# Layer 1's gate and up projections: seven block products in place of eight, from the fourth tile on

## The chip, the cores and the metric

One core of one Trainium2 chip runs the whole program in one launch. The metric is device microseconds of one execution; lower is better. The kernel before takes 1570.13 us (median of three runs, 1569.8 to 1570.21).

## What is computed

Two layers of a bidirectional backbone over 512 latent tokens (and, in layer 0, 256 context tokens), width 1024, all in f32. The change touches only the feed-forward block of layer 1, which works on the 512 latent tokens alone. Cut to that:

```python
D_MODEL, SEQ, D_FF = 1024, 512, 2816

def conv_ffn(h, w_gate, w_up, conv_w, conv_b, w_down):
    g = dwconv(h @ w_gate, conv_w, conv_b, FFN_CONV // 2, FFN_CONV // 2)   # 3 taps along the tokens
    return (jax.nn.silu(g) * (h @ w_up)) @ w_down

# layer 1, the last one
x   = layer_norm(ALPHA * x + m_x[2] * y_x, ln1_g[1], ln1_b[1])
f_x = conv_ffn(modulate(x, m_x[3], m_x[4]), ffn_w_gate[1], ffn_w_up[1], ffn_conv_w[1], ffn_conv_b[1], ffn_w_down[1])
x   = layer_norm(ALPHA * x + m_x[5] * f_x, ln2_g[1], ln2_b[1])
```

## The kernel before, in words

Matrix products keep f32 accuracy by splitting each operand into a high and a low part in a reduced f32 format and adding three products (high by high, high by low, low by high): `mm3`, lines 327 to 329. The activations of layer 1's feed-forward block are `h1h` and `h1l`, 128 partitions by 8 slices (k) by 512 tokens. Weights are loaded as f32 into `raw` (three buffers), cast to the high part on ScalarE (L146), and the low part is got by a subtraction on VectorE (L147); `wh` and `wl` have four buffers each. `units` is the list of weight panels in the order of their use; `split_to` and `use` walk it, and `dma_to` issues the loads on SyncE's queue in that order. The down panels are also multiplied by a row vector on VectorE (L152) before they are split (L153, L154).

The feed-forward block is cut into 22 tiles (t) of 128 hidden channels. A tile needs one gate panel and one up panel of 8 slices. In layer 1 each is one accumulation of 8 x 3 matmuls of 512 columns (`proj`), followed by the convolution over the tokens (two VectorE operations of 511 columns, L947 and L948, after a ScalarE copy out of PSUM, L946), Silu (L949), the product with up (L1776) and the split of the result into `a1` (L1703, L1704). Tiles are gathered in groups of 4, 4, 4, 4, 2 and 4 (`FG1`); the order `order2` is f0 to f4, down of group 0, f5 to f8, down of group 1, and so on, and last f19, f20, f21 and the down of group 5. A down of four tiles is eight accumulations of 4 x 3 matmuls of 512 columns, each added to the residual `R` on VectorE (L1792).

Before tile 0 stands the layer norm of the second half of the tokens, SB (`ln1_1(SB)`). While it runs, TensorE works on panels for the first half of the tokens (256 columns, `first_half`): six panels, those of tiles 0, 1 and 2. Their second halves follow when the layer norm's results are there.

Layer 0 has computed its gate and up projections by seven block products since tile 3 (`SW0 = 3`, `seven_tile`, L1119): the gate and up panels, each cut into two halves of the slices, are a 2 x 2 matrix of blocks, the activations, cut into two halves of the slices and two of the tokens, are another, and seven products of sums and differences of blocks give what eight products give. There a token half is 384 columns. Each product is 4 x 3 matmuls; seven VectorE additions (L1134) put the products together, a ScalarE copy (L1136) takes the first out, four GpSimd additions per tile (L373 to L376) make the weight sums, and `seven_acts` makes the activation sums once. The instruction order on each engine is made by a planner that goes by the order of the program and by its own costs; SyncE's order is the program's.

Of the kernel before, what the change touches and what calls it, by code (L numbers as in the profile page):

```python
# [15 lines left out]
KT = 8  # L16
S = 512
# [13 lines left out]
SW0 = 3  # L31
NH = T // 2
# [30 lines left out]
def tile_backbone(ctx, tc, x, cx, cols, mod_w, w_in, w_out, gates, w_qkv, na_out, bias, w_gate, w_up, w_down, rows, out):  # L63
# [296 lines left out]

    def seven_units(l, t):
# [85 lines left out]
    for o in order2:  # L447
        if o[0] == "f":
            gu_units(1, o[1])
# [527 lines left out]
    def seven_acts():  # L977


        t2, t3 = ([ytile().rearrange("p a n -> p (a n)").rearrange("p (k n) -> p k n", k=4) for _ in range(2)] for _ in range(2))  # L980
        t4 = [[Tp.tile([128, T], F32R, tag="t", name="t4", bufs=12).rearrange("p (k n) -> p k n", k=2) for _ in range(2)] for _ in range(2)]
        lo, hi = slice(0, NH), slice(NH, T)

        def dst(j, q, k):
            if j == 1:
                return (hh, hl)[q][:, k, hi]
            if j == 4:
                return t4[q][k // 2][:, k % 2, :]
            return (t2, t3)[j - 2][q][:, k, :]

        t1 = f(ytile().rearrange("p a n -> p (a n)").rearrange("p (k n) -> p k n", k=4))
        for k in range(4):
            fa, fb = Tt("fa"), Tt("fb")
            tt(out=fa, in0=f(hh[:, k, :]), in1=f(hl[:, k, :]), op=ALU.add)
            G.tensor_tensor(out=fb, in0=f(hh[:, k + 4, :]), in1=f(hl[:, k + 4, :]), op=ALU.add)
            tt(out=t1[:, k, :], in0=fa[:, hi], in1=fa[:, lo], op=ALU.subtract)
            tt(out=fa[:, hi], in0=fb[:, hi], in1=fa[:, hi], op=ALU.subtract)
            tt(out=fb[:, hi], in0=fb[:, hi], in1=t1[:, k, :], op=ALU.subtract)
# [6 lines left out]
        B["11"] = lambda q, k: (hh, hl)[q][:, k, lo]  # L1005
        B["21"] = lambda q, k: (hh, hl)[q][:, k + 4, lo]
        B["22"] = lambda q, k: (hh, hl)[q][:, k + 4, hi]
        seven["B"] = B
        yield
        for k in range(4):  # L1010
            nc.scalar.copy(dst(1, 0, k), t1[:, k, :])
            tt(out=dst(1, 1, k), in0=t1[:, k, :], in1=f(dst(1, 0, k)), op=ALU.subtract)
        yield

    seven = {}
    us = use(4, la=0)
# [23 lines left out]
    acts = seven_acts()  # L1040
# [700 lines left out]
    for u in units[state["use"] + 4:state["use"] + 6]:  # L1741
        u["pool"] = wp2
# [146 lines left out]
```

## Time and profile before

| | us |
|---|---|
| median of three runs | 1570.13 (1569.8 to 1570.21) |
| the profiled execution | 1569.22 |
| its span, first to last instruction | 1567.5 |
| TensorE busy in the span | 1528.1 (97%) |
| VectorE busy | 1158.0 (74%) |
| ScalarE busy | 766.7 (49%) |
| GpSimd busy | 320.2 (20%) |
| mean granted TensorE clock | 0.995 of full speed |

The last layer norm before the feed-forward block of layer 1 ends near 1214 us of the span, whole tiles run from about 1229 us on, and the last matmul starts at 1559.23 us. Between 1270 and 1540 us the profile shows TensorE busy without a break. The profile counts a matmul as busy from its start to its modelled end; successive matmuls overlap, so the distance from one start to the next, not the duration, is what one costs.

### The profile page before, as it was taken

Reading aid. Unit: us, or ns where it says so; the run is one execution under the profiler, and the core shown is the slowest. Engines: PE = TensorE matmul, PEld = TensorE weight load, DVE = VectorE, ACT = ScalarE, POOL = GpSimd, SP = SyncE. Lnnn points to the kernel's source line nnn. Section 1 sums busy time; section 2 is a strip of 40 time slices with the busy share of each in tenths; the row PEclk is TensorE's granted clock in tenths of the full one; section 3 lists DMA queues with packets and bytes.
Section 4 is the critical chain, followed back from the end, with each engine's and each line's share of the span. In section 5 each row is a group of like instructions: output and inputs, shape, how many; then the busy total and the mean of one; then the engine's idle time right before and its main releaser. Section 6 shows DMA issues by size and latency. Waiting matters only on the chain.

```text
span 1567.5 us, 24579 instructions
## 1 busy us (share of the span) xinstructions
PE 1528.1 (97%) x9508; PEld 1382.8 (88%) x9508; DVE 1158.0 (74%) x2061; ACT 766.7 (49%) x1309; POOL 320.2 (20%) x288
## 2 busy tenths in 40 slices
PE   7999999999999999999997999999999999999997
PEld 5888889998999999999997998989899988888886
DVE  5665556979999989877887678886787646555567
ACT  4555664775343232424455766666757523323232
POOL 0001113411413132234143122121236000000002
PEclk9999999999999999999998999999999999999999
DMA  9743437421443525322354233441154232333331
GB/s 310 234 143 105 140 115 222 134 61 52 128 142 100 158 90 173 96 70 68 96 153 142 68 115 102 124 139 54 57 149 141 94 94 81 107 91 108 97 94 54
DMA packets 259685, 184.25 MB, mean 118 GB/s; under 512 B 6640, under 2 KB 243824, under 8 KB 259568
## 3 DMA queue, kind: packets, MB, share of 16 engines
q1 hardware_dynamic: 259568, 182.68, 38.7%
q8 instruction: 75, 1.23, 0.3%
q14 instruction: 42, 0.34, 0.1%
HBM read 180.56 MB, written 2.10 MB: 117 GB/s over the span
## 4 chain that ended last, share of the span: by engine, by line
PE 78%; DVE 11%; DMA 4%; ACT 4%; issue 2%; POOL 1%; SPq 0%; POOLq 0%; DVEq 0%; ACTq 0%
PE ps L327 20%; PE ps L329 20%; PE ps L328 20%; PE ps L1790 3%; PE ps L1788 3%; PE ps L1789 3%; DMA mw<-in_mod_w_dram 2%; DVE wl L147 2%; PE ps L258 2%; DVE wa L1102 1%; PE ps L1404 1%; DVE ma L240 1%; ACT wh L146 1%; DMA raw<-in_w_out_dram 1%; DVE X L817 1%
## 5 line engine op out<-in xcount | busy, mean ns | idle before, releaser
L146 ACT CAST wh<-raw 128x1024 fp32r<-128x1024 f32 (+3 forms) x229 | 229.4, 1005 | 359.3 <-PE ps L328 159.1
L147 DVE TENSOR_TENSOR wl<-raw,wh 128x1024 fp32r<-128x1024 f32 (+3 forms) x229 | 275.5, 1205 | 112.8 <-ACT wh L146 111.6
L327 PE MATMUL ps<-hh,wh 128*128 128x256 f32 (+2 forms) x896 | 298.8, 334 | 1.1 <-ACT hh L883 1.1
L329 PE MATMUL ps<-hh,wl 128*128 128x256 f32 (+2 forms) x896 | 297.7, 333 | 2.2 <-DVE wl L147 2.2
L328 PE MATMUL ps<-hl,wh 128*128 128x256 f32 (+2 forms) x896 | 297.3, 332 | 0.0
L327 PE MATMUL ps<-a,wh 128*128 128x256 f32 (+2 forms) x784 | 247.4, 316 | 1.1 <-ACT wh L146 1.1
L329 PE MATMUL ps<-a,wl 128*128 128x256 f32 (+2 forms) x784 | 245.4, 313 | 1.9 <-DVE wl L147 1.8
L328 PE MATMUL ps<-a,wh 128*128 128x256 f32 (+2 forms) x784 | 245.2, 313 | 0.0
L327 PEld LDWEIGHTS ps<-hh,wh 128*128 128x128 f32 x896 | 170.0, 190 | 15.6 <-issue 4.1
L329 PEld LDWEIGHTS ps<-hh,wl 128*128 128x128 f32 x896 | 170.1, 190 | 13.6 <-DVE wl L147 3.1
L328 PEld LDWEIGHTS ps<-hl,wh 128*128 128x128 f32 x896 | 170.2, 190 | 9.8
L327 PEld LDWEIGHTS ps<-a,wh 128*128 128x128 f32 x784 | 149.9, 191 | 8.9 <-ACT wh L146 2.3
L329 PEld LDWEIGHTS ps<-a,wl 128*128 128x128 f32 x784 | 149.8, 191 | 8.4 <-DVE wl L147 2.7
L328 PEld LDWEIGHTS ps<-a,wh 128*128 128x128 f32 x784 | 149.8, 191 | 5.1
L327 PE MATMUL ps<-h1h,wh 128*128 128x512 f32 (+1 forms) x400 | 146.1, 365 | 0.0
L328 PE MATMUL ps<-h1l,wh 128*128 128x512 f32 (+1 forms) x400 | 145.3, 364 | 0.1
L329 PE MATMUL ps<-h1h,wl 128*128 128x512 f32 (+1 forms) x400 | 145.3, 364 | 0.0
L1391 POOL TENSOR_SCALAR s<-s,sm 128x512 f32<-128x512 f32 x64 | 50.6, 791 | 211.1 <-DVE sm L1390 187.5
L328 PEld LDWEIGHTS ps<-h1l,wh 128*128 128x128 f32 x400 | 75.4, 189 | 12.1 <-DVE h1l L886 0.3
L329 PEld LDWEIGHTS ps<-h1h,wl 128*128 128x128 f32 x400 | 75.4, 189 | 11.9
L327 PEld LDWEIGHTS ps<-h1h,wh 128*128 128x128 f32 x400 | 75.5, 189 | 11.7
L1733 POOL TENSOR_TENSOR R<-R,gb 128x512 f32<-128x512 f32 (+1 forms) x4 | 4.8, 1196 | 340.7 <-ACT R L1732 340.7
(278 smaller groups left out, 3194.7 us busy)
## 6 DMA issues: line engine op xcount, KB each, us to landing
raw<-in_w_gate_dram SPq DMA_DIRECT2D x44, 512.0 KB, 3.9
raw<-in_w_up_dram SPq DMA_DIRECT2D x44, 512.0 KB, 3.9
mw<-in_mod_w_dram SPq DMA_DIRECT2D x40, 384.0 KB, 4.5
a<-in_mod_w_dram SPq DMA_DIRECT2D x24, 512.0 KB, 5.5
raw<-in_w_out_dram SPq DMA_DIRECT2D x24, 512.0 KB, 4.8
raw<-in_w_qkv_dram SPq DMA_DIRECT2D x24, 512.0 KB, 4.3
raw<-in_w_down_dram SPq DMA_DIRECT2D x22, 512.0 KB, 3.6
raw<-in_w_down_dram SPq DMA_DIRECT2D x24, 448.0 KB, 4.1
```

Source lines behind the costliest of these rows:

```text
L146: nc.scalar.copy(h[:, :k], raw)
L147: nc.vector.tensor_tensor(out=l[:, :k], in0=raw, in1=f(h[:, :k]), op=ALU.subtract)
L240: stt(out=a[:, 0, :], in0=w, scalar=svec[:, k, 0:1], in1=a[:, 0, :], op0=ALU.mult, op1=ALU.add)
L258: mm(ps_rows[32 * g:32 * g + 32, :], mvec[:, 4 * i + g, :], t(g), start=(i == 0), stop=(i == n - 1), tile_position=(0, 32 * g))
L327: mm(acc, wh, rh, start=first, stop=False)
L328: mm(acc, wh, rl, start=False, stop=False)
L329: mm(acc, wl, rh, start=False, stop=last)
L817: stt(out=r, in0=ps_[:, 0:e - o], scalar=lco[:, row, vec, m:m + 1], in1=r, op0=ALU.mult, op1=ALU.add)
L1391: G.tensor_scalar(out=s, in0=s, scalar1=sm[:, 2:3], scalar2=0.0, op0=ALU.mult, op1=ALU.add)
L1788: mm(p, ah, u["h"][:, k % 2, :], start=k == 0, stop=False)
L1789: mm(p, ah, u["l"][:, k % 2, :], start=False, stop=False)
L1790: mm(p, al, u["h"][:, k % 2, :], start=False, stop=k == n - 1)
```

## The change

Layer 1 gets the same seven products from tile 3 on (`SW1 = 3`), with token halves of 256 columns. The weight units of a tile become gate, up, a sum of 512 columns (`ud`) and a sum of 1024 columns (`uc`), the last two without a load. `seven_acts` is made general and is also run for layer 1, in steps between tiles 0, 1 and 2; its sums need room, so `a1` lives in two buffers `ab` whose upper third holds some of them. The convolution becomes `tail1`, run in steps between the products of the next tile. Tile 2 is no longer done by halves: four first halves stand under the layer norm in place of six, and the pool `w2` goes. In the last down, the first three slices of four accumulations are done ahead of the fourth, which needs the last tile.

```diff
+SW1 = 3
+    z_mem = [lambda: Tp.tile([128, 512], F32, tag="mr", name="z", bufs=2)]
...
-            z = Tp.tile([128, 512], F32, tag="mr", name="z", bufs=2)
+            z = z_mem[0]()
...
-            gu_units(1, o[1])
+            (gu_units if o[1] < SW1 else seven_units)(1, o[1])
...
-    def seven_acts():
+    def seven_acts(h_, n, t2, t3, t4, t1, work, seven):
...
         for k in range(4):
+            fa, fb = work("fa"), work("fb")
+            tt(out=fa, in0=f(h_[0][:, k, :]), in1=f(h_[1][:, k, :]), op=ALU.add)
+            G.tensor_tensor(out=fb, in0=f(h_[0][:, k + 4, :]), in1=f(h_[1][:, k + 4, :]), op=ALU.add)
+            tt(out=t1(k), in0=fa[:, hi], in1=fa[:, lo], op=ALU.subtract)
             tt(out=fa[:, hi], in0=fb[:, hi], in1=fa[:, hi], op=ALU.subtract)
+            tt(out=fb[:, hi], in0=fb[:, hi], in1=t1(k), op=ALU.subtract)
             tt(out=fb[:, lo], in0=fb[:, lo], in1=fb[:, hi], op=ALU.subtract)
             for j, src in ((3, fa[:, hi]), (2, fb[:, hi]), (4, fb[:, lo])):
                 nc.scalar.copy(dst(j, 0, k), src)
                 tt(out=dst(j, 1, k), in0=src, in1=f(dst(j, 0, k)), op=ALU.subtract)
             yield
...
+        for k in range(4):
+            nc.scalar.copy(dst(1, 0, k), t1(k))
+            tt(out=dst(1, 1, k), in0=t1(k), in1=f(dst(1, 0, k)), op=ALU.subtract)
         yield
...
-    tap_p = opened("tap", bufs=3, side="right")
+    tap_p = opened("tap", bufs=6, side="right")
+    t4p = opened("T4", side="right")
+    t4b = t4p.tile([128, 2, 4, 256], F32R, name="t4b")
+    z_mem[0] = lambda: t4p.tile([128, 512], F32, tag="z", name="z", bufs=1)
+    ab = [hp.tile([128, 24, 256], F32R, tag="h", name="ab") for _ in range(2)]
+    t23b = [t[:, 16:24, :].rearrange("p (q k) n -> p q k n", q=2) for t in ab]
...
-            a1[gi] = hp.tile([128, 4, 2, S], F32R, tag="h", name="a1")
+            a1[gi] = ab[gi % 2][:, 0:16, :].rearrange("p (k q h) n -> p k q (h n)", k=4, q=2)
...
-    wp2 = opened("w2", bufs=2)
...
-    pf = [bank() for _ in range(6)]
...
-    for i in range(6):
-        fillq.append(first_half(i))
+    pf = [bank() for _ in range(4)]
+    for i in range(4):
+        fillq.append(mm_seg(pf[i][:, 0:256], us[i], 0, 256, h1H, h1L, range(KT)))
...
+    def tail1(t, ga, gb_, up):
+        tap = work1("tap")
+        w = lambda k: col("fcw1", 22 * k + t)
+        for p, o in ((ga, 0), (gb_, 256)):
+            act(out=tap[:, o:o + 256], in_=p, func=AF.Identity, scale=w(1), bias=col("fcb1", t))
+        yield
+        for p, c, o, n, k in ((ga, 0, 1, 256, 0), (gb_, 0, 257, 255, 0), (ga, 1, 0, 255, 2), (gb_, 0, 255, 256, 2)):
+            stt(out=tap[:, o:o + n], in0=p[:, c:c + n], scalar=w(k), in1=tap[:, o:o + n], op0=ALU.mult, op1=ALU.add)
+            if n == 255:
+                yield
+        act(out=tap, in_=tap, func=AF.Silu)
+        yield
+        tt(out=up, in0=tap, in1=up, op=ALU.mult)
+        yield
+        ffn1_out(t, up)
+        yield
+
+    def ffn1_seven(t):
+        g, up = work1("g"), work1("up")
+        def between(i):
+            tail_step(1)
+            if t in (3, 4) and i in (1, 4):
+                run_all(x_tok(2 * t - 6 + (i > 1)))
+        ga, gb_ = seven_tile(seven1["B"], 256, g, up, between)
+        tails.append(tail1(t, ga, gb_, up))
...
-    for t in range(3):
+    for t in range(2):
+        late_step(5)
...
+        ahead(1 + t)
         ffn1_out(t, tap)
+        next(acts)
+    for it in order2[2:]:
+            if t >= SW1:
+                ffn1_seven(t)
+                continue
...
-                us = use(n // 2, la=1)
+                us = use(n // 2, la=1 + hf)
...
                     down(us, i, hf)
+                    tail_step(1)
         else:
             us = use(n)
+            part = {}
+            for i in range(2):
+                for hf in range(2):
+                    part[i, hf] = down(us[hf * (n // 2):(hf + 1) * (n // 2)], i, hf, range(n - 1))
+                    tail_step(2)
+            while tails:
+                tail_step(1)
             for i in range(4):
                 for hf in range(2):
+                    down(us[hf * (n // 2):(hf + 1) * (n // 2)], i, hf, range(n - 1, n) if (i, hf) in part else None, part.get((i, hf)))
                     final_sums(i, hf)
                 final(i)
```

## Rows read from the trace of the kernel before

**Rows 1.** The page: busy time by engine, and the chain by engine.

```profile
PE 1528.1 (97%) x9508; PEld 1382.8 (88%) x9508; DVE 1158.0 (74%) x2061; ACT 766.7 (49%) x1309; POOL 320.2 (20%) x288
...
PE 78%; DVE 11%; DMA 4%; ACT 4%; issue 2%; POOL 1%; SPq 0%; POOLq 0%; DVEq 0%; ACTq 0%
```

**Rows 2.** Busy time by stretch (PE, PEld, DVE, ACT, POOL, granted clock, DMA): layer 1's tiles.

```profile
1270.00:1400.00 130.00, 130.00 (x576) 107.68 (x575) 70.04 (x80) 40.42 (x48) 0.00 (x0) 1.00 0.32 97
1400.00:1540.00 140.00, 140.00 (x619) 115.99 (x618) 78.93 (x91) 45.24 (x54) 0.00 (x0) 1.00 0.30 91
```

**Rows 3.** Timeline of TensorE (start, duration, instruction): matmuls of 512 columns.

```profile
1298.64 0.39 PE L329 MATMUL ps<-h1h,wl 128*128 128x512 f32 x1
...
1300.00 0.39 PE L329 MATMUL ps<-h1h,wl 128*128 128x512 f32 x1
```

**Rows 4.** Timeline of TensorE: matmuls of 256 columns under the layer norm.

```profile
1204.14 0.28 PE L327 MATMUL ps<-h1h,wh 128*128 128x256 f32 x1
...
1210.14 0.28 PE L329 MATMUL ps<-h1h,wl 128*128 128x256 f32 x1
```

**Rows 5.** Busy time by stretch: layer 0's seven-product tiles of 384 columns.

```profile
688.00:760.00 72.00, 72.00 (x416) 71.84 (x415) 53.91 (x86) 31.22 (x40) 27.69 (x18) 1.00 0.22 66
```

**Rows 6.** VectorE's groups in 1240 to 1540 (busy us, mean ns, idle before).

```profile
L147 DVE TENSOR_TENSOR wl<-raw,wh 128x1024 fp32r<-128x1024 f32 x34 | 41.5, 1221 | 27.9 <-ACT wh L146 27.5
...
L154 DVE TENSOR_TENSOR wl<-raw,wh 128x1024 fp32r<-128x1024 f32 x21 | 25.7, 1224 | 21.9 <-ACT wh L153 17.4 <-PE ps L1710 3.6
L152 DVE TENSOR_TENSOR raw<-raw,m5b 128x1024 f32<-128x1024 f32 x19 | 23.2, 1224 | 28.3 <-DMA raw<-in_w_down_dram 28.3
L948 DVE SCALAR_TENSOR_TENSOR tap<-ps,colt,tap 128x511 f32<-128x511 f32 x18 | 13.5, 748 | 0.5
...
L1704 DVE TENSOR_TENSOR a<-tap,a 128x512 fp32r<-128x512 f32 x19 | 13.0, 684 | 0.0
```

**Rows 7.** VectorE's groups in 688 to 760, layer 0.

```profile
L1134 DVE TENSOR_TENSOR g<-ps,g 128x384 f32<-128x384 f32 x10 | 5.5, 547 | 0.0
...
L1170 DVE SCALAR_TENSOR_TENSOR tap<-ps,colt,tap 128x255 f32<-128x255 f32 x8 | 3.8, 479 | 0.1
```

**Rows 8.** Timeline of VectorE and GpSimd in one seven-product tile of layer 0.

```profile
707.25 2.56 DVE L1170 SCALAR_TENSOR_TENSOR tap<-ps,colt,tap 128x384 f32<-128x384 f32 x6 [1.55 <-ACT tap L1167]
...
715.17 0.54 DVE L1134 TENSOR_TENSOR g<-ps,g 128x384 f32<-128x384 f32 x1
715.64 0.55 DVE L1134 TENSOR_TENSOR ps<-ps,g 128x384 f32<-128x384 f32 x1
...
706.93 1.30 POOL L374 TENSOR_TENSOR raw<-raw 128x512 f32<-128x512 f32 x1
712.08 1.88 POOL L375 TENSOR_TENSOR raw<-z,raw 128x512 f32<-128x512 f32 x1 [3.86 <-DVE wl L147]
```

**Rows 9.** The page: loads of the up panels (count, size, us to landing).

```profile
raw<-in_w_up_dram SPq DMA_DIRECT2D x44, 512.0 KB, 3.9
```

**Rows 10.** Timeline around the layer norm ahead of layer 1's tiles.

```profile
1199.71 1.23 DVE L147 TENSOR_TENSOR wl<-raw,wh 128x1024 fp32r<-128x1024 f32 x1 [0.57 <-ACT wh L146]
...
1202.39 1.56 PE L871 MATMUL ps<-sq,ones 128*128 128x256 f32 x6 [1.11 <-POOL sq L864]
...
1211.96 0.36 PE L327 MATMUL ps<-h1h,wh 128*128 128x256 f32 x1
...
1213.15 0.76 DVE L886 TENSOR_TENSOR h1l<-h,h1h 128x256 fp32r<-128x256 f32 x2 [0.38 <-ACT h1h L883]
```

**Rows 11.** Busy time in tiles 1 and 2, and one VectorE row of layer 0's activation sums.

```profile
1221.00:1230.00 9.00, 9.00 (x74) 8.88 (x73) 8.75 (x11) 4.97 (x7) 0.00 (x0) 1.00 0.49 167
...
378.18 1.62 DVE L997 TENSOR_TENSOR fa<-fb,fa 128x384 f32<-128x384 f32 x1 [1.08 <-POOL fb L995]
```

**Rows 12.** Busy time by stretch around a pause of TensorE in layer 0's last layer norms.

```profile
832.00:836.00 4.00, 0.60 (x3) 0.40 (x3) 2.79 (x2) 2.89 (x6) 4.00 (x5) 0.69 0.64 187
836.00:840.00 4.00, 4.00 (x17) 3.82 (x18) 0.00 (x0) 0.00 (x0) 0.53 (x1) 0.50 0.62 189
```

More of the change, by code (lines that the diff above doesn't have):

```diff
@@ L1004, in seven_acts, with acts0 @@
         B = {j: (lambda q, k, j=j: dst(j, q, k)) for j in (1, 2, 3, 4)}
-        B["11"] = lambda q, k: (hh, hl)[q][:, k, lo]
-        B["21"] = lambda q, k: (hh, hl)[q][:, k + 4, lo]
-        B["22"] = lambda q, k: (hh, hl)[q][:, k + 4, hi]
+        B["11"] = lambda q, k: h_[q][:, k, lo]
+        B["21"] = lambda q, k: h_[q][:, k + 4, lo]
+        B["22"] = lambda q, k: h_[q][:, k + 4, hi]
         seven["B"] = B
-        yield
         for k in range(4):
-            nc.scalar.copy(dst(1, 0, k), t1[:, k, :])
-            tt(out=dst(1, 1, k), in0=t1[:, k, :], in1=f(dst(1, 0, k)), op=ALU.subtract)
+            nc.scalar.copy(dst(1, 0, k), t1(k))
+            tt(out=dst(1, 1, k), in0=t1(k), in1=f(dst(1, 0, k)), op=ALU.subtract)
         yield
     seven = {}
+    def acts0():
+        t23 = [[ytile().rearrange("p a n -> p (a n)").rearrange("p (k n) -> p k n", k=4) for _ in range(2)] for _ in range(2)]
+        t4 = [[Tp.tile([128, T], F32R, tag="t", name="t4", bufs=12).rearrange("p (k n) -> p k n", k=2) for _ in range(2)] for _ in range(2)]
+        t1 = f(ytile().rearrange("p a n -> p (a n)").rearrange("p (k n) -> p k n", k=4))
+        yield from seven_acts((hh, hl), NH, lambda q, k: t23[0][q][:, k, :], lambda q, k: t23[1][q][:, k, :], lambda q, k: t4[q][k // 2][:, k % 2, :],
+                              lambda k: t1[:, k, :], Tt, seven)
     us = use(4, la=0)
@@ L1756, in tile_backbone, with work1, t1_ @@
     fill_all()
-    for t in range(3):
-        tap = tap_p.tile([128, S], F32, tag="tap", name="tap")
-        late_step(4)
+    def work1(name):
+        return tap_p.tile([128, S], F32, tag="tap", name=name)
+    seven1 = {}
+    t1b = {}
+    def t1_(k):
+        if k not in t1b:
+            t1b[k] = l_tile("h32", 256)
+        return t1b[k]
+    acts = seven_acts((h1h, h1l), 256, lambda q, k: t23b[0][:, q, k, :], lambda q, k: t23b[1][:, q, k, :], lambda q, k: t4b[:, q, k, :], t1_, work1, seven1)
+    def tail1(t, ga, gb_, up):
[23 more added lines that the diff above has]
+    for t in range(2):
+        tap = work1("tap")
+        late_step(5)
         run_all(mm_seg(pf[2 * t][:, 256:512], us[2 * t], 256, 512, h1H, h1L, range(KT)))
@@ L1763, in tile_backbone @@
         tt(out=tap, in0=tap, in1=pf[2 * t + 1], op=ALU.mult)
+        ahead(1 + t)
         ffn1_out(t, tap)
[L1765 removed]
+        next(acts)
+    for it in order2[2:]:
         if it[0] == "f":
             t = it[1]
[L1768 to L1770 removed]
+            if t >= SW1:
+                ffn1_seven(t)
+                continue
+            tap = work1("tap")
+            late_step(len(late))
+            (p,) = proj(use(la=1), (XS,), h1H, h1L)
+            next(acts)
             conv_ffn(1, t, tap, XS, p)
[L1772 to L1775 removed]
+            (p,) = proj(use(la=3), (XS,), h1H, h1L)
+            next(acts)
             tt(out=tap, in0=tap, in1=p, op=ALU.mult)
             ffn1_out(t, tap)
+            next(acts)
             continue
@@ L1781, in tile_backbone, with down @@
         last = gi == len(groups1) - 1
-        def down(us, i, hf):
-            p = bank()
-            for k in range(n):
+        def down(us, i, hf, ks=None, p=None):
+            p = p or bank()
+            for k in ks or range(n):
                 u = us[k // 2]
@@ L1790, in down @@
                 mm(p, al, u["h"][:, k % 2, :], start=False, stop=k == n - 1)
+            if k < n - 1:
+                return p
             r = R[:, i, 512 * hf:512 * hf + 512]
```

33 lines of the change are left out of this document (4 added, 29 removed).

## The prediction

> **What bounds the kernel now.** I read the page first: TensorE is busy 97% of the span and holds 78% of the chain that ended last, and the three matmul lines share it [rows 1]. Then the busy time by stretch: from 1270 to 1540 us TensorE is busy all the time at full clock, while VectorE works 54 to 56%, ScalarE about 31% and GpSimd nothing [rows 2]. So in layer 1's tiles the number of matmuls and the distance between them set the time, and three engines have room. The third view is TensorE's timeline, for that distance: six matmuls of 512 columns in 1.36 us, 0.2267 us each [rows 3]; fifty of 256 columns, each with weights of its own, in 6.00 us, 0.1200 us each [rows 4]. Half the columns cost 53%, not 50%. Last come VectorE's groups, because the change loads that engine most.
>
> **The products.** A tile of 2 x 8 x 3 = 48 matmuls of 512 columns costs 48 x 0.2267 = 10.88 us. Seven products of 4 x 3 matmuls of 256 columns are 84 x 0.1200 = 10.08 us. An eighth of the columns goes (1.36 us), and 0.56 us of it is paid back because 84 short matmuls carry more fixed cost than 48 long ones. **0.80 us a tile, 19 tiles (3 to 21): -15.2 us.** That products of four slices keep their spacing is shown by layer 0: 416 matmuls, nearly all of 384 columns, in 72.00 us, 0.173 each, which is what the line through the other two sizes gives [rows 5].
>
> **VectorE in a tile.** A group's mean overlaps its neighbour: two additions of 0.54 and 0.55 start 0.47 apart [rows 8], so I take 0.08 off each. Weight splits: three of 1024 columns at 1.15 and one of 512 at 0.60 (the price of the 512-column L1704) [rows 6]: 4.05. Seven additions of 256 columns: 384 columns cost 0.547 [rows 7] and 512 cost 0.684 [rows 6], so 256 some 0.41, spaced 0.33: 2.3. Four convolution steps of 255 or 256 columns at 0.479 [rows 7], spaced 0.40: 1.6. Product and split of the result, 0.60 each: 1.2. Together 9.2 us in 10.08, where before it was some 5 in 10.88. That is 91%, against 75% in layer 0's tiles, which keep TensorE full [rows 5]. Its queue waits for others: 1.55 us ahead of the convolution in a layer 0 tile [rows 8]. If VectorE falls behind, such waits shrink first, since what it waits for is then ready. The tightest operands that I find: `uc`'s low part is wanted at the fourth product, 4.56 us into the tile; its buffers come free at the tile's start, cast and subtraction take 2.3 (the cast taken like the subtraction), VectorE's queue 0.8 to 1.3, so it is there at 3.1 to 3.6. The next `ub`'s low part is wanted at 11.76 us; its buffers come free after the fifth product at 7.2, 2.3 and some 1.2 of queue make 10.7. Both have a microsecond. So inside a run of tiles I charge nothing, with 0 to 1 us a tile as bounds; the upper end is a rival below.
>
> **GpSimd and SyncE.** Four additions a tile, 1.30 to 1.88 each [rows 8], 5.2 to 7.5 us in 10.08 on an idle engine [rows 2]: hidden. The next up load waits for the split of the up panel before it; load 3.9 us [rows 9], two additions 2.6, cast and subtraction 2.3, so 8.8 us round a loop that has 10.08. That holds only while the additions stay near 1.30; at 1.88 it is 10.0. The loads keep their number and order; only this wait on SyncE's queue is new, and the gate load behind it has a tile to spare.
>
> A GpSimd addition of the same size took 1.30 us in one place and 1.88 in another, beside a VectorE operation with two SBUF inputs [rows 8]. The Trainium skill, "GPSIMD Engine Reference", section "8. Key points", says that GpSimd shares its SBUF interfaces with VectorE and contends with VectorE instructions that have two SBUF inputs. It speaks against this change, which puts four such additions beside weight splits that all have two; the trace agrees with it. By the row nothing is added to the sum; by the page's rule, if VectorE pays as well, the VectorE rival below comes out.
>
> **Six first halves become four.** Before, 144 matmuls of first halves fill the layer norm of SB; about 56 of them run after the variance product at 1202.39 and carry TensorE to the second halves, which start at 1211.96, just as the operands arrive (the last at 1213.9) [rows 10]. Now there are 96, so eight are left after the variance product; TensorE runs dry and follows the layer norm: the first gate half ends at 1214.3 in place of 1211.96 + 2.88 = 1214.8. Then three halves of 2.88 and a whole tile 2 of 10.88 follow, 19.5 us, where five halves of 2.88 stood, 14.4. Tile 3 begins 4.6 us later. Two weight splits on VectorE (the row at 1199.71 and one like it [rows 10]) no longer stand in the layer norm's way, worth 0 to 2.3 us; I take 1.4. **+3.2 us (2 to 5).**
>
> **The activation sums.** They need all tokens, so VectorE can begin them only when the layer norm is done, near 1212.5 with that gain. Per slice pair one operation of 512 columns and seven of 256: 0.60 + 7 x 0.33 = 2.9; four of them 11.7, of which the last 0.7 can come late. Beside that lie four splits before the second product of tile 3, 4.6, and the convolution of tiles 0 to 2 with L948's 0.748 [rows 6], six at 0.67 and four of 0.60, 6.4. Sum 22.0 us, with 21.3 until tile 3's second product: 0.7 late. The third product needs 1.9 to 3.8 us more work 1.7 us later: 0.9 to 2.8 late. This part of VectorE is nearly full already before the change: 8.75 of 9.00 us from 1221 on; and next to GpSimd a subtraction of layer 0's sums took 1.62 us, normally 0.55, after waiting 1.08 for it [rows 11]. **+3 us (1 to 6).**
>
> **From tiles to a down.** The last tile before a down replaces the next tile's splits (2.9) by two down panels scaled and split, 4 x 1.15 [rows 6]: 10.9 us, wanted 11.6 us after the tile's start. Half a microsecond of room, five times; **+2 us (0 to 4)**. In the down VectorE has twice the time that it needs and catches up.
>
> **The end.** The last down needs four panels early: 15.5 us of VectorE by 13.7 us after tile 21's start, and the tail of tile 21 behind them. The three-slice parts give 36 x 0.2267 = 8.2 us of cover for that tail, which needs about as much. **+2 us (0.5 to 4).**
>
> **The clock.** In layer 0 TensorE paused, 0.60 us busy in 4, and in the next 4 us the granted clock was 0.50 of full speed, the lower of the two levels (1.2 GHz) [rows 12]: 17 matmuls in place of the 33 that 0.12 us each would allow [rows 4], so 2 us lost. The two pauses above may be long enough; **+1 us (0 to 4)**.
>
> Sum: -15.2 + 3.2 + 3 + 2 + 2 + 1 = -4.0. The profiled execution, 1569.2 us (span 1567.5 and 1.7 around it), becomes 1565.2; the median of the runs lies 0.9 above it, so **1566 us**.
>
> **The rivals.** *Nothing waits but the layer norm:* the planner fills VectorE's holes, as it does in layer 0's tiles, and only the 3.2 us are paid: -12, 1558 (1556 to 1562). For it: no wait of TensorE in layer 0's tiles [rows 5]. Against it: 75% there, 91% here.
> *The pauses cost double:* both lower the clock and each down is late by 0.8 us: 4 to 5 us more, 1571 (1569.5 to 1574), the same as before.
> *VectorE sets the tile, slower than before:* its 9.2 us plus waits that don't shrink pass 10.08 us. It decides from 0.9 us of lengthening a tile. If each of four GpSimd additions costs VectorE 0.5 us (above, one cost it 1), a tile takes 11.2, 1.1 too much; over 19 tiles, less what the downs absorb, some 8 to 20 us: 1577 (1574 to 1586). For it: rows 11's 1.62 us and rows 8's 1.88. Against it: in layer 0's tiles GpSimd works 27.69 of 72 us beside VectorE and TensorE is still never idle [rows 5].
> *The change doesn't gain what it says:* spacing of 0.1295 us would make 84 matmuls as long as 48 long ones; then only the losses stay, about 1580. Nothing in rows 4 or 5 points there.
>
> **How the numbers follow.** Forecast (1562.5 to 1569.5) 0.45; nothing waits 0.20; double pauses 0.18; VectorE 0.14; no gain 0.03. About 0.2% (3.1 us) is what a measurement of this kernel can tell from no change: faster is below 1567.0, slower above 1573.3. Faster: 0.20 and two thirds of 0.45, 0.50. Same: the other third and most of 0.18, 0.30. Slower: 0.14, 0.03 and 0.03 of the double pauses, 0.20. For eight times in ten the range leaves out the lower 0.07 of "nothing waits", 0.10 of the VectorE case and 0.03: 1558 to 1575.
>
> **What would show it.** In the changed profile: 12 matmuls of 256 columns every 1.44 us in a tile; a pause of 2 to 4 us before 1214, another at tile 3's second or third product with a VectorE releaser; VectorE near 90% in the runs of tiles with TensorE still unbroken; a clock below 1.00 near the pauses. Wrong would be pauses of TensorE at every tile with L147 as releaser (VectorE sets the tile), or none at all.

## The result and the profile after

The changed kernel takes 1598.34 us (median of four runs, 1596.11 to 1600.38); the kernel before, beside it, 1569.97. The ratio is **1.0171, 95% interval 1.0158 to 1.0184**: 28 us slower, where 1566 was forecast. Differences behind a ratio are taken in later sections as the ratio's part of 1570 us, since the kernel before took 1570 us in one series and 1572 to 1573 in others.

The page of the changed kernel, to be read beside [rows 1]:

```profile
span 1594.2 us, 26381 instructions
PE 1525.7 (96%) x10144; PEld 1403.8 (88%) x10144; DVE 1283.3 (80%) x2306; ACT 814.0 (51%) x1401; POOL 458.8 (29%) x368
```

TensorE's busy time hardly moved, VectorE's and GpSimd's grew. The rest is read by stretch. Three borders are on TensorE's timeline of both kernels: the variance product of layer 1's last layer norm in front of the tiles, the first matmul of the first down projection, and that of the last one. The kernel before, its two down projections (L1788):

```profile
1254.67 0.39 PE L1788 MATMUL ps<-wh,a 128*128 128x512 f32 x1
1537.55 0.39 PE L1788 MATMUL ps<-wh,a 128*128 128x512 f32 x1
```

and the changed kernel, variance product (L874) and down projections (L1836):

```profile
1204.13 0.59 PE L874 MATMUL ps<-sq,ones 128*128 128x256 f32 x2
1271.95 0.40 PE L1836 MATMUL ps<-wh,ab 128*128 128x512 f32 x1
1556.08 0.40 PE L1836 MATMUL ps<-wh,ab 128*128 128x512 f32 x1
```

With the variance product of before at 1202.39 [rows 10] and the ends of the spans, 1567.5 and 1594.2:

| stretch, us | before | after | |
|---|---|---|---|
| up to the variance product | 1202.4 | 1204.1 | +1.7 |
| **start**: to the first down | 52.3 | 67.8 | +15.5 |
| **groups**: first down to last down, tiles 5 to 21 | 282.9 | 284.1 | +1.2 |
| **end**: last down to the span's end | 30.0 | 38.1 | +8.1 |

So 17 tiles with 0.8 us less of matmuls each brought nothing in the groups, and start and end lost 24 us besides. Busy time in the groups, two runs of four tiles, each with the down behind it (columns as in [rows 2]):

```profile
1295.14:1337.40 42.26, 41.23 (x337) 40.41 (x336) 37.02 (x60) 20.59 (x30) 20.89 (x12) 1.00 0.31 89
1337.40:1361.42 24.02, 22.43 (x99) 17.88 (x98) 20.82 (x27) 8.01 (x10) 6.99 (x4) 1.00 0.37 109
1361.42:1402.57 41.15, 40.71 (x338) 40.30 (x336) 36.84 (x60) 20.58 (x30) 21.16 (x12) 1.00 0.30 90
1402.57:1426.57 24.00, 22.38 (x99) 17.87 (x97) 20.85 (x27) 8.02 (x10) 7.30 (x4) 1.00 0.36 110
```

A run of four tiles takes 41.15 us where 40.3 was the sum of its matmuls (4 x 10.08), a down 24.0 where its 96 matmuls of 0.2267 make 21.76. VectorE works 36.8 of 41.2 us in a run, which is the 9.2 a tile of the prediction, but 20.8 of 24.0 in a down, for which the prediction gave it twice the time that it needs. TensorE's waits in this stretch (us in total, times, longest):

```profile
PE ps L1837 <- DVE wl L155: 4.2, 4, 1.1
PE ps L330 <- DVE wl L148: 2.8, 6, 0.8
PE ps L1836 <- ACT wh L154: 1.7, 3, 0.6
```

L153 to L155 scale and split the down panels (L153 and L155 on VectorE, the cast L154 on ScalarE), L148 subtracts for the low part of the other panels: it is mostly VectorE's queue that TensorE waits for, above all at the downs.

### The profile page after: what moved, and what is told of

It reads as the page before. It is cut to its first block, busy times and chain, and to the rows that moved or that the text cites. A ratio compares the mean times of both kernels' runs of the same rounds, so it can differ in the third digit from the quotient of the medians.

```text
span 1594.2 us, 26381 instructions
## 1 busy us (share of the span) xinstructions
PE 1525.7 (96%) x10144; PEld 1403.8 (88%) x10144; DVE 1283.3 (80%) x2306; ACT 814.0 (51%) x1401; POOL 458.8 (29%) x368
## 3 DMA queue, kind: packets, MB, share of 16 engines
q1 hardware_dynamic: 259568, 182.68, 38.1%
## 5 line engine op out<-in xcount | busy, mean ns | idle before, releaser
L147 ACT CAST wh<-raw 128x1024 fp32r<-128x1024 f32 (+3 forms) x248 | 249.1, 1008 | 326.6 <-PE ps L329 149.6
L148 DVE TENSOR_TENSOR wl<-raw,wh 128x1024 fp32r<-128x1024 f32 (+3 forms) x248 | 304.4, 1231 | 107.8 <-ACT wh L147 107.1
L376 POOL TENSOR_TENSOR z<-raw 128x512 f32<-128x512 f32 x38 | 55.8, 1467 | 337.9 <-DMA raw<-in_w_up_dram 284.5
L328 PE MATMUL ps<-h1h,wh 128*128 128x256 f32 (+1 forms) x384 | 110.9, 292 | 3.7 <-ACT h1h L886 2.0
L330 PE MATMUL ps<-h1h,wl 128*128 128x256 f32 (+1 forms) x384 | 111.4, 292 | 1.6 <-DVE wl L148 1.6
L329 PE MATMUL ps<-h1l,wh 128*128 128x256 f32 (+1 forms) x384 | 110.8, 291 | 0.1
L378 POOL TENSOR_TENSOR raw<-z,raw 128x512 f32<-128x512 f32 x38 | 60.8, 1599 | 140.6 <-DVE wl L148 93.0
```

Source lines behind the costliest of these rows:

```text
L147: nc.scalar.copy(h[:, :k], raw)
L148: nc.vector.tensor_tensor(out=l[:, :k], in0=raw, in1=f(h[:, :k]), op=ALU.subtract)
L328: mm(acc, wh, rh, start=first, stop=False)
L329: mm(acc, wh, rl, start=False, stop=False)
L330: mm(acc, wl, rh, start=False, stop=last)
L376: G.tensor_tensor(out=z, in0=quarter(u, 0), in1=quarter(u, 1), op=ALU.add)
```

## The experiments

Kernels e1 to e8 are the changed one with one edit each; e9 to e12, e14 and e15 build on one another, and e13 is the kernel before with one edit. The stretches are read from each kernel's own trace as above; each stands for one execution, the median for several. Line numbers shift by a few from kernel to kernel, and `...` marks a cut in an edit.

| kernel | start | groups | end | median us | ratio to before (95%) |
|---|---|---|---|---|---|
| before | 52.3 | 282.9 | 30.0 | 1570.0 | 1 |
| changed | 67.8 | 284.1 | 38.1 | 1598.3 | 1.0171 (1.0158 to 1.0184) |
| e1 eight products | 55.7 | 282.9 | 32.7 | 1581.7 | 1.0047 (1.0030 to 1.0063) |
| e2 no activation sums | 52.8 | 282.2 | 39.2 | 1585.8 | 1.0077 (1.0062 to 1.0092) |
| e3 no weight sums | 59.2 | 269.7 | 36.9 | 1575.9 | 1.0016 (1.0005 to 1.0027) |
| e4 late operations on ScalarE | 64.6 | 281.8 | 39.7 | 1596.3 | 1.0144 (1.0128 to 1.0159) |
| e5 sums unused | 70.7 | 284.9 | 37.8 | 1603.6 | 1.0190 (1.0175 to 1.0205) |
| e6 no scaling | 67.9 | 275.3 | 32.9 | 1585.0 | 1.0074 (1.0057 to 1.0090) |
| e7 plain end | 68.1 | 283.2 | 30.3 | 1590.1 | 1.0103 (1.0084 to 1.0122) |
| e8 seven from tile 5 | 56.2 | 282.6 | 38.0 | 1582.0 | 1.0061 (1.0046 to 1.0076) |
| e9 e7 + e8 + one bank | 55.4 | 283.9 | 30.1 | 1578.5 | 1.0036 (1.0018 to 1.0054) |
| e10 eight behind the downs | 56.2 | 279.4 | 30.3 | 1575.7 | 1.0017 (1.0007 to 1.0027) |
| e11 two banks again | 56.2 | 278.0 | 30.1 | 1572.7 | 1.0004 (0.9995 to 1.0013) |
| e12 six first halves | 52.3 | 278.4 | 29.8 | 1572.0 | 0.9997 (0.9988 to 1.0007) |
| e13 before + layer 0's step | 52.3 | 282.9 | 30.0 | 1576.3 | 1.0024 (1.0012 to 1.0036) |
| e14 layer 0 restored | 52.3 | 277.9 | 29.7 | 1567.9 | 0.9972 (0.9961 to 0.9983) |
| e15 eight ahead of the downs | 52.3 | 274.0 | 30.4 | 1567.4 | **0.9969 (0.9956 to 0.9981)** |

**Is it the products and their side work, or the structure around them?**

```diff
-SW1 = 3
+SW1 = 22
...
-        next(acts)
```

> The changed kernel with its restructuring (four first halves instead of six, deeper tap buffers, the last tile's product left for the end in the first two rows of the last down projection), but with eight block products in every tile, and so without activation sums, weight sums and tails. Theory A (the loss comes from the seven products' side work on GpSimd and VectorE): the structure costs what the prediction charged, 3 to 6 us, so 1573 to 1576 us against 1570 before. Theory C (the restructured start and end cost most of the loss, the products gain little): 1585 us or more, with the start of the first down projection and the end after the last down as late as in the changed kernel (end of 38 us against 30).

Measured: 7 us slower than before; 3.4 in the start, nothing in the groups, 2.7 in the end. By the ratio that is 1577 us beside a kernel before of 1570, between the theories and near A: structure is a quarter of the loss. The start's 3.4 us are a wait of TensorE of 2.0 us for the layer norm (ScalarE's h1h) and 4 us at a granted clock of 0.60 behind it, with 24 matmuls in place of some 36 (fence in the last section).

**The two kinds of sums.** In e2 the seven products read the activations as they are; in e3 the further weight panels are the loaded ones:

```diff
+        seven1["B"] = {j: (lambda q, k, j=j: (h1h, h1l)[q][:, k + 4 * (j // 3), half[j % 2]]) for j in (1, 2, 3, 4)}
...
+    acts = no_acts()
```

> The changed kernel without the activation sums: the seven products read parts of the normalised activations as they are, so the result isn't the reference's; products, weight sums and tails stay. Theory A1 (the 15.6 us that the start lost come from the activation sums, which stand behind late residual operations and weight sums in GpSimd's queue and behind splits in VectorE's and ScalarE's): the first down starts 9 to 13 us earlier, 1586 to 1590 us against 1598. Theory A2 (the start's loss is the clock and the deeper weight loads): within 4 us of 1598.

```diff
+            if l == 1:
+                units[i + 2]["raw"] = g["raw"][:, 0:4, :]
+                units[i + 3]["raw"] = g["raw"]
+                return
             z = z_mem[0]()
```

> The changed kernel without layer 1's four GpSimd additions per tile that form the summed weight panels; the two further panels are split from the loaded gate and up panels as they are, so the result isn't the reference's; all VectorE and ScalarE work, the activation sums and the products stay. Theory A (GpSimd's sums hold back VectorE, whose splits and products took 1.3 to 1.9 times as long in places, and stand in a chain load, sums, cast, split): 10 to 18 us less, 1580 to 1588 us; VectorE's split of the third panel back from 1.0 to 0.68 us and the GpSimd waits of ScalarE gone. Theory B (VectorE's own amount of work sets the tile): at most 4 us less, 1594 or more.

Without the activation sums the start is 52.8 us, 15 less than in the changed kernel, and the other stretches move by 2 us at most. Without the weight sums the groups fall to 269.7 us, 13.2 less than before: the products' gain, nearly the 13.6 of 17 tiles at 0.80. In the start the weight sums matter too: with activation sums alone it is 59.2. The same two stretches as above, a run and a down, of e3:

```profile
1349.68:1389.88 40.20, 40.20 (x337) 40.20 (x336) 33.98 (x61) 20.68 (x30) 0.00 (x0) 1.00 0.33 100
1389.88:1411.67 21.79, 21.79 (x98) 18.03 (x97) 17.74 (x25) 7.92 (x10) 0.00 (x0) 1.00 0.36 107
```

TensorE is full, and VectorE, with one or two instructions more or less at the borders, is busy 33.98 us instead of 36.84 and 17.74 instead of 20.85. Which of its operations grew shows in its groups (busy us, mean ns). The changed kernel, end of the first down to start of the last:

```profile
L148 DVE TENSOR_TENSOR wl<-raw,wh 128x1024 fp32r<-128x1024 f32 x49 | 64.6, 1322 | 21.9 <-ACT wh L147 21.9
L1784 DVE TENSOR_TENSOR up<-tap,up 128x512 f32<-128x512 f32 x15 | 19.1, 1276 | 0.0
L148 DVE TENSOR_TENSOR wl<-z,wh 128x512 fp32r<-128x512 f32 x17 | 16.9, 996 | 5.3 <-ACT wh L147 5.3
L1139 DVE TENSOR_TENSOR g<-ps,g 128x256 f32<-128x256 f32 x34 | 14.0, 412 | 0.0
```

and e3:

```profile
L148 DVE TENSOR_TENSOR wl<-raw,wh 128x1024 fp32r<-128x1024 f32 x49 | 59.5, 1220 | 22.8 <-ACT wh L147 22.8
L148 DVE TENSOR_TENSOR wl<-raw,wh 128x512 fp32r<-128x512 f32 x17 | 11.6, 684 | 5.3 <-ACT wh L147 5.3
L1788 DVE TENSOR_TENSOR up<-tap,up 128x512 f32<-128x512 f32 x16 | 10.9, 683 | 0.0
L1143 DVE TENSOR_TENSOR g<-ps,g 128x256 f32<-128x256 f32 x34 | 14.2, 417 | 0.6 <-PE ps L330 0.6
```

Operations with both operands in SBUF grew (the product with up from 683 to 1276 ns, the 512-column split from 684 to 996), those with one operand in PSUM (`ps`) didn't. The scaling of the down panels (L153), also with two operands in SBUF, grew only from 1216 to 1241 ns; of 18 such operations 4 fall beside a GpSimd addition. What decides is whether a GpSimd operation runs at the time. Four rows of the changed kernel: the product with up without one, an addition of GpSimd, and beside it an addition of VectorE with an operand in PSUM and the product with up again:

```profile
1403.64 0.68 DVE L1784 TENSOR_TENSOR up<-tap,up 128x512 f32<-128x512 f32 x1
1387.81 2.34 POOL L377 TENSOR_TENSOR raw<-raw 128x512 f32<-128x512 f32 x1
1388.93 0.41 DVE L1139 TENSOR_TENSOR g<-ps,g 128x256 f32<-128x256 f32 x1
1389.27 1.43 DVE L1784 TENSOR_TENSOR up<-tap,up 128x512 f32<-128x512 f32 x1
```

Sorted in this way from first down to last, the product takes 0.68 us in the 4 places without GpSimd and 1.52 in the 12 with it; the addition L1139 takes 0.41 in either case (10 places and 24). GpSimd pays as well; its sums in the changed kernel (same stretch as the groups above), where [rows 8] have 1.30 us for one beside a VectorE operation with an operand in PSUM:

```profile
L377 POOL TENSOR_TENSOR raw<-raw 128x512 f32<-128x512 f32 x16 | 31.0, 1938 | 1.3
L379 POOL TENSOR_TENSOR raw<-raw 128x512 f32<-128x512 f32 x16 | 30.9, 1931 | 1.3
```

The Trainium skill, "SBUF — State Buffer", section "Who interferes with whom", states just that division: a VectorE instruction with two SBUF inputs contends with a GpSimd instruction that reads SBUF; one with at most one SBUF input, outside the 2-port perf modes, doesn't. The trace agrees: 1.52 us against 0.68 for the one kind, 0.41 on both sides for the other.

**Growth or wait?** e3 takes away both GpSimd's presence and the chain load, sums, cast, split. e5 keeps the presence alone:

```diff
+                for a, b in ((quarter(u, 0), quarter(u, 1)), (quarter(g, 0), quarter(u, 0)), (quarter(u, 1), quarter(g, 0)), (quarter(g, 1), quarter(g, 0))):
+                    G.tensor_tensor(out=z, in0=a, in1=b, op=ALU.add)
+                return
```

> The changed kernel in which GpSimd still does four additions of the same size per tile on the loaded panels, but into a scratch tile that nobody reads; the further panels are split from the loaded ones as they are, so the result isn't the reference's. It has GpSimd's presence in the memory, and not the chain load, sums, cast, split. Without the sums at all the groups of tiles took 269.7 us and the kernel some 24 us less than the changed one. Theory A-contention (the loss in the groups is VectorE's operations made longer by GpSimd's): groups of 279 to 284 us, as in the changed kernel (284.1), time within 6 us of it. Theory A-chain (the loss is the wait for the sums): groups of 270 to 273 us, 1574 to 1582 us.

Groups of 284.9 us, a little above the first range: as long as with the chain, longer than without GpSimd by 15.2. One run and one down of e5:

```profile
1366.76:1407.81 41.05, 40.71 (x337) 40.30 (x336) 36.46 (x60) 21.20 (x30) 21.13 (x12) 1.00 0.31 91
1407.81:1431.81 24.00, 22.40 (x99) 17.87 (x98) 22.41 (x27) 7.92 (x10) 7.75 (x5) 1.00 0.37 109
```

So the loss in the groups is contention, not the chain. e6 asks whether VectorE is really what TensorE waits for, by taking other work from it:

```diff
-                         scale=lambda u, hf=hf: m5b[:, hf * 512:(hf + 1) * 512].unsqueeze(1).to_broadcast([128, 2, 512]))
```

> The changed kernel without the scaling of the down panels (22 VectorE multiplications of 1.22 us), so the result isn't the reference's; weight sums, activation sums and products stay. Theory B' (VectorE is full in tiles and downs once GpSimd stretches it, so any work taken from it comes back as time): the downs return to 21.8 to 22.3 us from 24.0 and the runs of four tiles lose up to 0.8 us, so 9 to 14 us less in all, 1584 to 1590 us. If VectorE is not the bound but only the chain through GpSimd is: at most 3 us less.

The time fell by 15 us, at the expectation's edge:

```profile
1361.71:1402.85 41.14, 40.73 (x337) 40.32 (x336) 36.90 (x60) 22.76 (x33) 20.98 (x12) 1.00 0.33 102
1402.85:1424.82 21.97, 21.97 (x98) 17.95 (x97) 16.08 (x22) 5.82 (x8) 6.36 (x4) 1.00 0.34 97
```

Downs at 21.97 with GpSimd's 6.36 us still beside them; the end is 5.2 us shorter too. The runs of tiles, in which nothing is scaled ahead of their last tile, didn't move, against the second half of the expectation. In the downs VectorE is the bound, and it can give way to GpSimd only where it has room.

**The start and the end.** Of what the prediction named as signs, VectorE near 90% in the runs, a pause ahead of 1214 us and a lower clock behind it came; but tile 3's pauses had another releaser than VectorE. GpSimd's timeline in the changed kernel's tiles 2 and 3:

```profile
1226.65 1.48 POOL L993 TENSOR_TENSOR fb<-h1h,h1l 128x512 f32<-128x512 f32 x1
1228.13 9.00 POOL L842 TENSOR_SCALAR X<-X,colt 128x256 f32<-128x256 f32 x6
1237.10 1.44 POOL L993 TENSOR_TENSOR fb<-h1h,h1l 128x512 f32<-128x512 f32 x1
1238.49 1.26 POOL L378 TENSOR_TENSOR raw<-z,raw 128x512 f32<-128x512 f32 x1
1239.84 1.32 POOL L379 TENSOR_TENSOR raw<-raw 128x512 f32<-128x512 f32 x1
1241.12 1.44 POOL L993 TENSOR_TENSOR fb<-h1h,h1l 128x512 f32<-128x512 f32 x1
```

Six late residual operations (L842) stand between two adds of the activation sums (L993) and the weight sums that tile 3 needs (L378, L379). ScalarE's queue stands behind the last of these, and TensorE behind ScalarE (its longest waits from the variance product to the first down):

```profile
1241.19 1.04 ACT L147 CAST wh<-raw 128x1024 fp32r<-128x1024 f32 x1 [3.89 <-POOL raw L379]
```

```profile
PE ps L328 <- ACT wh L147: 4.3, 2, 3.9
PE ps L328 <- ACT h1h L886: 2.0, 1, 2.0
PE ps L328 <- ACT R L1722: 1.7, 1, 1.7
PE ps L329 <- DVE ab L1000: 1.5, 1, 1.5
```

Around these pauses the granted clock fell, to the lower of its two levels behind the longest one:

```profile
1244.00:1248.00 4.00, 3.19 (x15) 3.19 (x16) 4.00 (x8) 2.31 (x5) 0.00 (x0) 0.50 0.03 8
```

e4 moves the late operations, e8 gives the sums more time:

```diff
-        late_step(5)
+        late_step(5, True)
...
-            late_step(len(late))
+            late_step(len(late), True)
```

> The changed kernel, complete, with the layer norm's late residual operations (scale and shift of 16 blocks) on ScalarE instead of GpSimd. Theory A1 (those operations, 1.5 us each beside VectorE instead of 0.54, block GpSimd's queue ahead of the activation sums' adds and the weight sums): 4 to 9 us less, 1589 to 1594 us. If they only wait beside something longer: within 3 us of 1598, or slower as ScalarE's casts stand behind them.

```diff
-SW1 = 3
+SW1 = 5
...
+        if t:
+            next(acts)
```

> The changed kernel, complete, with seven products from tile 5 on instead of tile 3, and the five steps of the activation sums spread over tiles 1 to 4. Theory A1 (at the start the activation sums are too much for one tile and a half beside late residual operations and weight sums): from the variance product to the first down 56 to 59 us instead of 67.8, with 1.6 us of gain given up inside that; 1587 to 1590 us. If the activation sums cost their time wherever they stand: 65 us or more, no change in time.

```diff
-            if t >= SW1:
+            if SW1 <= t < NF - 1:
...
-                    down(us[hf * (n // 2):(hf + 1) * (n // 2)], i, hf, range(n - 1, n) if (i, hf) in part else None, part.get((i, hf)))
+                    down(us[hf * (n // 2):(hf + 1) * (n // 2)], i, hf)
```

> The changed kernel, complete, with its last tile by eight products and the last down projection row after row as before the change, with nothing held back. Theory C-end (the end's 8.2 us come from the held back products and the last tile's tail, which leave the rows' final operations to VectorE in one heap): the stretch from the last down to the end falls from 38.1 to 30 to 32 us, and the tile before it costs 0.8 us more: 1590 to 1592 us. If the end is late for the panels' splits alone: 35 us or more.

In e8, tile 4's up product, and in e7, both products of tile 21 read a quarter of their input where the fourth activation sum has overwritten it; the instructions and sizes are those of the whole computation. e4 gained 3.2 us in the start and 4 in all, at the foot of its range, and the intervals of e4 and the changed kernel just overlap. With the late operations out of GpSimd's queue TensorE waits in tile 3 for VectorE, which works there on the activation sums without a gap ahead of the split:

```profile
PE ps L330 <- DVE wl L148: 6.1, 2, 3.5
```

So the late operations alone were not the start's loss. e8's start is 56.2 (A1 right, 17 us in all by the ratios, more than expected), e7's end 30.3 (C right; 11 us in all by the ratios, of which the end shows 7.8). e8 also takes the weight sums of tiles 3 and 4 out of the start and spreads the late operations, four to a tile. So the start's loss is too much work in one place, not the sums as such.

**Putting together a version that gains.** e9 takes e7 and e8, with the fourth sum in memory of its own, and tries to relieve VectorE by one bank for both gate halves:

```diff
+        pg = bank() if pg else None
+        ga = product(ua, 1, "21", None if pg is None else pg[:, lo])
...
+        gb_ = product(uc, 1, "22", None if pg is None else pg[:, hi])
```

> A complete version put together from what the runs before showed: seven products from tile 5 to tile 20, activation sums spread over tiles 1 to 4 with their fourth part in memory of its own, the last tile by eight products and the last down row after row, and gate halves of a tile in one bank so that the two taps of the convolution are two VectorE operations of 511 columns instead of four of 256. GpSimd's weight sums and the panels' scaling stay. If the terms add: from the variance product to the first down 56 to 58 us, groups 280 to 283 us (downs still 24), end 30 to 32 us, in all 1571 to 1577 us where before is 1570 to 1573. If VectorE's relief by the two taps is enough to cover GpSimd's stretching: groups of 274 us and 1565 us.

Start and end came out as the terms said, or a little better; the groups did not gain (283.9 us), and the time, 1578.5, is above both ranges. A new wait took the place of the relief, TensorE ahead of the second half for VectorE's addition into the first:

```profile
PE ps L328 <- DVE ps L1139: 4.9, 11, 0.8
```

e10 is e9 with eight products in the first tile behind each down too:

```diff
-SW1 = set(range(5, 21))
+SW1 = set([t for t in range(6, 21) if t not in (9, 13, 17, 19)])
```

> The version before with eight products also in the first tile after each down projection (tiles 5, 9, 13, 17, 19 and 21), so that GpSimd has no weight sums to do for a tile during a down; eleven tiles are left with seven. Theory A-contention with VectorE full: downs of 21.8 to 22.3 us, runs of four tiles 41.1 to 41.8 us, so groups of 274 to 278 us against 282.9 before the change; start 56 to 58, end 30 to 32 us: 1563 to 1568 us, faster than before by 0.2 to 0.5%. If the downs stay at 24 us it is the down panels' own scaling and splits, not GpSimd: 1573 us.

e11 takes e9's edit on the banks out of e10 again:

```diff
-        gb_ = product(uc, 1, "22", None if pg is None else pg[:, hi])
+        gb_ = product(uc, 1, "22")
```

> The version with eight products beside the downs, with the gate halves of a tile in two banks again and four VectorE operations for the taps. With one bank TensorE waited three times 1.6 us for VectorE's addition into the first half before it could write the second. If that was all that kept the groups at 279.4 us: groups of 274 to 276 us, downs of 21.8 us, 1566 to 1569 us, faster than before by 0.2 to 0.4%. If four operations bring VectorE back to its limit: groups of 278 to 281 us and 1572 to 1575 us.

e10 brought 4.5 us in the groups, not the 6 to 10 expected. e11, with two banks, brought 1.5 more and missed its 274 to 276: its waits for `ps` are gone, but a down takes 22.64 us, not 21.8, with waits of 0.6 for the scaled panel's cast. Neither came near the time that was expected of a gain; e11's fits its second range, VectorE at its limit. e12 is e11 with six first halves, and so with tile 2 by halves again:

```diff
-    pf = [bank() for _ in range(4)]
+    pf = [bank() for _ in range(6)]
```

> The version with two banks, and six first halves ahead of the layer norm's end instead of four, as before the change (the two further panels' splits in memory of the down projection's second buffer, free until tile 4). The loss at the start that the runs with eight products showed is 3.4 us. If it comes from the two first halves: from the variance product to the first down 52.3 to 53.5 us instead of 56.2, and 3 to 4 us less than the version with two banks, 1562 to 1566 us, faster than before by 0.4 to 0.6%. If it comes from the activation sums: no change against that version.

The start is 52.3 us, exactly as before the change, with the activation sums in it: the two first halves were its whole remaining loss. But the median did not follow (0.9997). In its trace e12 makes up 4.7 us on the kernel before from the variance product on, and it reaches that product 5.1 us later (1207.5 us of the span). Ahead of it only one line of the change moves work: in layer 0 a `yield` is gone between the first three activation sums and the fourth.

```diff
         seven["B"] = B
-        yield
         for k in range(4):
```

This alone, on the kernel before, is e13:

> The kernel before, complete, with one part of the change alone: layer 0's fourth activation sum is split in the same step as the first down's second panel instead of one step later. If this moved step is what brings all variants late to layer 1: 1 to 3 us slower than before, with waits of TensorE for layer 0's residual additions (0.5 and 0.2 us) in its first down projection, where before has none. If the lateness is scatter: within 0.5 us of before.

```diff
         seven["B"] = B
+        if t5 is None:
+            yield
```

This, on e12, is e14 (`t5` is given in layer 1 only):

> The version with six first halves, complete, with layer 0's activation sums in the steps that they had before the change. If the moved step costs 1 to 3 us: 1569 to 1571 us where the version before it had 1572.0 and the kernel before 1572.2, so 0.1 to 0.2% faster than before. If it is scatter: the same ratio as that version, 0.9997.

e13 is 0.24% slower than before, 3.8 us (1.9 to 5.7), and e14, which takes it back, is better than e12 by 0.25 points. In layer 0's first down, e13 waits where the kernel before only has the first of these three, with 0.9 us:

```profile
PE ps L329 <- DVE wl L147: 1.1, 1, 1.1
PE ps L327 <- DVE Xc L817: 0.5, 1, 0.5
PE ps L327 <- DVE X L817: 0.2, 1, 0.2
```

These make 0.9 us more of waits. TensorE's matmuls, followed one by one against the kernel before, fall behind by 1.5 us between 382 and 388 us of the span. All the kernels with the moved step fall behind there, eleven of them by 1.4 to 1.7 us; e1, e2 and e5, in which the granted clock falls behind the same waits (0.66 to 0.91 from 388 to 396 us, 1.00 in the others), by 3.0 to 3.2. e14 and e15, with the step restored, lose 0.1. So the loss and its place are shown; its size is 3.8 us by the times, with a wide interval, and 1.4 to 3.2 by the traces, and the difference stays open. The 5.1 us of e12's trace are not the step's price: e14 reaches the variance product 3.6 us later than before as well, and single executions of kernels with the same layer 0 reach it between 1201.6 (e7) and 1209.7 us (e1). Nor does the step tell why e12's median is only 1 us better than e11's, with a start 3.9 us shorter: both have it. The intervals leave room for 3 us there.

e15 is e14 with the eight products moved to the other side of the downs:

```diff
-SW1 = set([t for t in range(6, 21) if t not in (9, 13, 17, 19)])
+SW1 = set([5, 6, 7, 9, 10, 11, 13, 14, 15, 17, 19, 20])
```

> The version with layer 0's steps restored, complete, with eight products in the last tile ahead of each down projection (8, 12, 16, 18 and 21) instead of the first behind it; twelve tiles have seven. GpSimd's sums for the first tile of a run then lie beside the down, and no tail does. If the tail and the late scaling of the down panels are what is left there: downs of 21.8 to 22 us, groups of 274 to 277 us against 278.4, 1 to 4 us less than the version with eight behind the downs. If GpSimd beside the down is: downs of 22.7 us or more, and the same time or up to 3 us more.

Twelve tiles keep seven products, and each tile ahead of a down has eight:

```profile
1343.90:1385.22 41.32, 41.26 (x302) 39.15 (x300) 37.19 (x59) 21.38 (x31) 13.50 (x8) 1.00 0.36 110
1385.22:1406.98 21.76, 21.76 (x98) 18.02 (x96) 14.43 (x16) 5.45 (x6) 6.89 (x4) 1.00 0.29 84
```

The downs are free of waits with GpSimd's 6.89 us in them; VectorE has only 14.43 of 21.76 us to do there. Groups of 274.0 us, as the first theory had it, are 8.8 less than before, of 9.6 that twelve tiles can give. This version is **0.31% faster than before** (0.19 to 0.44), 1567.4 us. It and e14 can't be told apart by time, only by their groups.

## Why the prediction was wrong, point by point

- **The products, -15.2:** right. e3 shows 13.2 us for 17 tiles, 0.78 each.
- **VectorE in a tile, 0 (0 to 1 a tile):** the 9.2 us came true (36.84 / 4), but by chance: alone it is 8.5 (33.98 / 4), and 0.7 is what GpSimd adds. The runs took 177.0 us where 17 tiles at 10.08 are 171.4: +5.6, inside the bounds, above the value.
- **From tiles to a down, +2 (0 to 4):** mis-sized, and the sentence "in the down VectorE has twice the time that it needs and catches up" failed. Most of the last tile's tail, four scalings and splits, eight additions and the next tile's first splits make 17.7 us, GpSimd's sums stretch them to 20.8. The downs took 9.2 us more. With the runs this is 14.8, where e3 and e5 measure 14.5 and 15.2 for GpSimd's presence.
- **GpSimd hidden, 0:** this is the step on which the forecast fell. It asked whether GpSimd had the time for its sums, and put what they take from VectorE at nothing: 14.5 us in the groups (e3). The rival "VectorE sets the tile" had the mechanism, [rows 11] and [rows 8] spoke for it, and its price of 0.5 us for each addition was near: (36.84 - 33.98 + 20.85 - 17.74) / 16 = 0.37, and 0.33 over the whole groups (248.0 us of VectorE against 225.6 in e3, 68 additions). It had the place wrong: a tile takes 10.3 us, not 11.2, and the downs pay; its 1577 fell short too, for start and end. What spoke against it, layer 0's full TensorE [rows 5], was read from a stretch in which VectorE had 25% free. Over the whole of layer 0's tiles and downs, 400 to 830 us, the trace of before has three waits of TensorE for VectorE's split, two of them behind stretches in which VectorE was full and GpSimd at work; the longest (columns as in [rows 2]):

```profile
PE ps L329 <- DVE wl L147: 2.4, 3, 1.5
544.00:552.00 8.00, 8.00 (x48) 7.63 (x47) 8.00 (x10) 1.43 (x2) 5.67 (x4) 1.00 0.32 90
552.00:560.00 8.00, 6.48 (x38) 6.16 (x37) 7.71 (x10) 1.88 (x2) 2.48 (x2) 1.00 0.29 93
```

These rows spoke for the rival, and the prediction did not ask for them.

- **Six first halves to four, +3.2 (2 to 5):** the size was right (e1: +3.4, e12 takes all of it back), in part by luck: it is 2.0 us of wait and some 1.5 of clock, which stood under another term. Where the clock held, in e2, the wait is nearly all.
- **The activation sums, +3 (1 to 6):** alone they cost 4.7 us (e3's 59.2, against 54.5: the 52.3 of before, less 1.6 for two tiles, plus 3.8 for the wait and the clock that e3 has at the same place). With the weight sums in the same queues it is some 8.6 more. The step left out that L378 and L379, the late operations and the sums' adds share GpSimd's one queue; and with that queue relieved VectorE is late all the same (e4).
- **The end, +2 (0.5 to 4):** 8.1. The last down's four held-back sums leave VectorE's additions and the rows' final operations for one heap, behind panels that it still has to scale; e7, without them, gets 7.8 back, and e6, without the scaling, 5.2.
- **The clock, +1 (0 to 4):** the pauses of the start lowered it to between 0.50 and 0.86 in five of the stretches of 4 us from 1204 us on; that loss is inside the start's.
- **Layer 0:** not in the sum at all. The opening says that the change touches only layer 1's feed-forward block; it also moves a step of layer 0, which alone costs 3.8 us by the times (1.4 to 3.2 by the traces).

Together: products right, three terms (downs with runs, start, end) short by some 13, 10 and 6 us, and one missing.

## What to carry to other kernels

Work given to an idle GpSimd isn't free if VectorE works from SBUF beside it: count VectorE's stretched time stage by stage, and put such sums where it has room. Here a down with 14.43 us of VectorE in 21.76 lost nothing to them, one with 20.85 in 24.00 lost 2.2 us. A saving on TensorE that is bought with side work pays only in the stages with room for that work; used in twelve tiles, with start and end as before the change, it gained, used in all nineteen with everything at once it lost. And a helper that a change shares with an earlier stage is part of the change: one moved step there cost nearly as much (3.8 us by the times) as the final version gains (4.9).

## What the runs showed of the hardware

The same pause had two outcomes for the clock. In e1 and e2 TensorE waits 2.0 us at the same place, with the same matmuls ahead of it (columns as in [rows 2]); e1:

```profile
1213.00:1217.00 4.00, 1.87 (x13) 1.47 (x12) 3.97 (x11) 3.69 (x9) 2.17 (x2) 0.97 0.00 0
1217.00:1221.00 4.00, 4.00 (x24) 4.00 (x23) 2.53 (x7) 3.60 (x10) 4.00 (x6) 0.60 0.00 0
```

e2:

```profile
1212.00:1216.00 4.00, 1.87 (x14) 1.47 (x13) 3.92 (x12) 3.69 (x10) 2.44 (x2) 1.00 0.00 0
1216.00:1220.00 4.00, 4.00 (x36) 4.00 (x35) 2.40 (x6) 3.35 (x9) 4.00 (x6) 1.00 0.00 0
```

Behind one pause the granted clock was 0.60 of full speed (2.4 GHz), so mostly the lower level, and 12 matmuls fewer were done in 4 us; behind the other it stayed full. Twelve kernels' traces have this pause, the changed one and e1 to e11: in ten the granted clock behind it is 0.60 to 0.71 for 4 us, in e2 and e9 it stays full. What decides between the two wasn't found. A pause of this length is a risk, and a comparison of two single executions can carry 1.5 us of it.
